# Sharing the split of a weight block between context and latent columns, moving the scans, and moving residual additions to VectorE

## The chip, the cores and the metric

The kernel runs on one core of a Trainium2 chip. Its time is the device time of one execution in microseconds (us). Five engines work from queues of their own and meet at semaphores: TensorE (PE, with the weight load PEld), VectorE (DVE), ScalarE (ACT), GpSimd (POOL) and SyncE (SP), which issues most DMA transfers. A queue runs in order: an instruction that waits holds up all that stand behind it.

## The reference

One layer of a hybrid block over 2048 latent tokens of width 1024, with a prefix of 256 context tokens that shares the weights. The parts that the change touches:

```python
hc = modulate(rms_norm(ctx, g_pre_mix[l]), sm_c, cm_c)           # 256 context tokens
_, _, xs_c, B_c, C_c, dt_c = mixer_inputs(hc, w_in[l], ..., full=False)
y_c, hf_c, hb_c = ssd_bidir(xs_c, B_c, C_c, dt_c, ..., h0, h0, False)   # gives the start states
hx = modulate(rms_norm(x, g_pre_mix[l]), sm_x, cm_x)             # 2048 latent tokens
uf_x, z_x, xs_x, B_x, C_x, dt_x = mixer_inputs(hx, w_in[l], ..., full=True)
y_x, _, _ = ssd_bidir(xs_x, B_x, C_x, dt_x, ..., hf_c, hb_c, True)
x = x + gm_x * rms_norm(mixer_output(...), g_post_mix[l])
hx2 = modulate(rms_norm(x, g_pre_ffn[l]), sf_x, cf_x)
x = x + gf_x * rms_norm(swiglu(hx2, w_gate[l], w_up[l], w_down[l]), g_post_ffn[l])
```

`mixer_inputs` multiplies by `w_in` and passes the x, B and C columns through a convolution of seven taps along a row. The scan of the latent tokens starts from the final states of the context.

## The kernel before, in words

**Numbers.** A float32 product is made of three fast matmuls: each factor is split into a high part (`hi`, a cast) and a low part (`lo`, the subtraction of the high part), and hi·hi, hi·lo and lo·hi are summed in PSUM. So each weight block costs a load of 512 KB (`wload`, tile `raw`, four buffers), a cast and a subtraction (`wparts`, which names the engines).

**Projection (some 90 to 720 us).** Tokens come in three sections: 0 and 1 are the two halves of the latent tokens (1024 each), 2 is the context (256). The list `blocks` holds, in order, which 128 columns (kind z, u, x, B, C or dt, and number) are multiplied for which section. A block of section 0 or 1 is 48 matmuls of 512 columns, one of section 2 is 24 of 256. While block n is multiplied, `want` loads the weights of block n+2, and when it ends `finish_block` starts their split and the block's own chain (`column_block`: convolution on VectorE, Silu on ScalarE, transposes on TensorE, a store). When one of the next two blocks is of the context, the low part is made on VectorE, and a latent block's cast too; otherwise the low part is on GpSimd and the cast on ScalarE. PSUM has three places for blocks, handed round in turn; a place is free when the convolution has read it.

Side chains run between the matmuls, set in order by a planner (`Pace`): each step of a chain has a due time in planned TensorE time and is written into the queues when that time has come; `drain` writes the rest of a chain at once. Such chains are: `dt_section` (the step sizes of a section, some twenty short VectorE instructions), `scan_steps` (states from chunk to chunk; section 2 first, its end state starts section 0), `section_chain` (loads, normalizes and modulates 512 rows of section 1), `ada_steps` and `fourier_steps`.

**FFN.** Gate and up products follow, then `down`: two passes p of seven positions each. A position is 11 blocks of 12 matmuls; `down_parts` makes each block's two operands (`wd` and `hd`, a cast on ScalarE and a subtraction on VectorE each), four blocks ahead. In the product numbered 6, `block(11)` is first replaced in place by `block(12)` minus `block(11)`. `finish` scales four row tiles and adds the residual rows, in eight pairs of half tiles, beside the following position; it runs three times (pass 0 position 6, pass 1 positions 0 and 5). From the second gate and up pass on, the order of each queue is made by the compiler's list scheduler, not by hand.

Of the kernel before, what the change touches and what calls it, by code (L numbers as in the profile page):

```python
# [17 lines left out]
ALU = mybir.AluOpType  # L18
# [12 lines left out]
XB, BB, CB, ZB = 6, 4, 4, 6  # L31
# [133 lines left out]
def fourier_ssd_block(ctx, tc, a):  # L165
# [624 lines left out]
    def group(kind, sec):  # L790
        return [(kind, j, sec) for j in range({"z": ZB, "u": 2, "x": XB, "B": BB, "C": CB}[kind])]

    c_, light = group("B", 2) + group("x", 2), group("z", 0)[4:] + group("u", 0)
    blocks = group("z", 0)[:4] + [("dt", 0, 2)]
    for i, blk in enumerate(light + group("B", 0)):
        blocks += c_[i : i + 1] + [blk]
    blocks += c_[8:]
    x_ = group("x", 0)
    blocks += x_[:5] + [("dt", 0, 0)] + x_[5:] + group("C", 0)
    u_, b_, x_, z_ = group("u", 1), group("B", 1), group("x", 1), group("z", 1)  # L800
    cl = group("C", 1)
    blocks += u_ + [("dt", 0, 1)] + b_ + x_
# [6 lines left out]

    wraw, wq = {}, {}  # L810

    def want(bi):
        if bi < len(blocks) and blocks[bi][0] != "dt":
            kind, j, sec = blocks[bi]
            c0 = off[kind] + j * P
            wraw[bi] = wload(w_in[:, :, c0 : c0 + P], [P, KD, P])

    def split(bi, *engines, **where):
        if bi in wraw:
            wq[bi] = wparts(wraw.pop(bi), [P, KD, P], *engines, **where)  # L820
        yield

# [115 lines left out]
    def down_parts(p, i, f):  # L938

        hpos[1] = (7 * p + i) * ((NJ + 1) // 2) + f // 2  # L940
        hidden_loads(3 if f % 2 == 0 else 2)

        def block(b):
            return wblock[p, (b, f // 4)][:, f % 4]

        def temp():
            return ta[0].tile([P, 512], F32, tag="ws", name="wt", bufs=4)

        def sub(engine, out, x, y):
            engine.tensor_tensor(out, x, y, op=ALU.subtract)  # L950
            return out

        i_ = ORDER[p][i]
        if i_ in (1, 5):
            src = block(11)
        elif i_ in (2, 3):
            src = block({2: 21, 3: 22}[i_])
        elif i_ == 6:
            sub(G, block(11), block(12), block(11))
            src = sub(V, temp(), block(22), block(11))  # L960
        elif i_ == 7:
            src = sub(G, temp(), block(22), block(12))
        else:
            src = sub(G, temp(), block(11), block(22))
            V.tensor_tensor(src, src, block(21), op=ALU.add)
        w = wp.tile([P, 2, 512], F32R, tag=("hi", "lo")[pos[1] % 2], name="wd")
        S.copy(w[:, 0], src)
        sub(V, w[:, 1], src, w[:, 0].bitcast(F32))
        raw = hraw[7 * p + i, f // 2][:, f % 2]
        tag, bufs = (("xt", 2), ("sg", 3))[pos[1] // 2 % 2]  # L970
        h = ta[0].tile([P, 2, 512], F32R, tag=tag, name="hd", bufs=bufs)
        S.copy(h[:, 0], raw)
        sub(V, h[:, 1], raw, h[:, 0].bitcast(F32))
        return w, h
# [427 lines left out]
    with tc.manual_schedule(engines=ordered):  # L1402
# [136 lines left out]
        def when(ready, gen):  # L1539
            while not ready():  # L1540
                yield 0.5
            yield from gen

        def settled(kinds, sec):
            return all(b in chains and chains[b].done for b in range(2, nblk) if blocks[b][0] in kinds and blocks[b][2] == sec)

        def finish_block(bi, ps):
            kind, j, sec = blocks[bi]
            live = [chains[b] for b in plain if b in chains and not chains[b].done and (blocks[b][2] == 2) == (sec == 2)]
            pace.drain(*live[:-1])  # L1550
            two = after(bi, 2)
            brief = two < nblk and any(blocks[b][2] == 2 for b in (after(bi, 1), two))
            splits[two] = pace.start(split(two, *((V, V) if brief and blocks[two][2] != 2 else (V,) if brief else (G,))))
            chains[bi] = pace.start(column_block(kind, j, sec, ps.rearrange("p a b -> p (a b)"), lambda: read.add(bi)))
# [11 lines left out]
        while bi < nblk:  # L1566
            kind, j, sec = blocks[bi]
            if kind == "dt":
                pace.drain(*[chains[b] for b in chains if blocks[b][0] == "dt"])
                if sec == 0:  # L1570
                    pace.drain(scan[2])
                chains[bi] = pace.start(dt_section(acts[sec], sec, place(bi), lambda bi=bi: read.add(bi)))
                pace.due()
                bi += 1
                continue
            want(after(bi, 2))
            pace.drain(splits[bi])
            pace.now = max(pace.now, splits[bi].t)
            if (kind, j, sec) == ("x", 1, 0):
                prep1[0] = pace.start(section_chain(0, lambda: True))  # L1580
            if (kind, j, sec) == ("C", 0, 0):
                pace.drain(prep1[0])
                prep1[1] = pace.start(section_chain(1, lambda: 1 in begun))
            if bi == first1:
                b1 = after(bi, 1)
                want(after(bi, 3))
                pz = [place(bi), place(b1)]
                pace.drain(splits[b1])
                for i, b in ((0, bi), (0, b1), (1, bi), (1, b1)):
                    if i == 1 and b == bi:  # L1590
                        pace.drain(prep1[1])
                    for k in range(KD):
                        project_step(pz[b - bi], wq[b], acts[1][i], i, k)
                        pace.due()
                    if i == 1:
                        finish_block(b, pz[b - bi])
                fnet = pace.start(when(lambda: settled("u", 1), fourier_steps()))
                late.append(pace.start(when(lambda: fnet.done, load_wo(0, "B"))))
                bi += 2
                continue  # L1600
            if bi == plain[-3]:
                pace.window = None
                pace.drain(ada)
                pace.drain(*[chains[b] for b in chains if blocks[b][0] != "z"], scan[1])
                places[1] = 1
                vacate("y")
                begin_outputs()
                pend.append(chunk_loads(NCH - 1, False))
                front = pace.start(chunk_front(pend[0]), 5.0)
                wts = pace.start(when(lambda: fnet.done, late_steps()), 1.0)  # L1610
            if bi == plain[-2]:
                pace.hurry = True
                pace.drain(*late)
                wo_raw.extend(wo_load(1, kp) for kp in range(KD // 2))
            if bi == plain[-1]:
                pace.due()
                pace.drain(fnet, front, wts)
                wo1 = load_wo(1, "C")
            if after(bi, 1) == first1:
                ps = project(bi, wq.pop(bi), acts[sec], lambda: begun.update({1: True}))  # L1620
            elif bi == plain[-1]:
                ps = project(bi, wq.pop(bi), acts[sec], beside=wo1)
            else:
                ps = project(bi, wq.pop(bi), acts[sec])
            finish_block(bi, ps)
            if kind == "x" and j == XB - 1:
                scan[sec] = pace.start(when(lambda sec=sec: settled("xB", sec), scan_steps(sec)), 8.0)
            bi += 1
        fourier_split(pend[0])
        pace.window = None  # L1630
# [219 lines left out]
    def finish(p, r, o, sq):  # L1850

        ss = ta[0].tile([P, 4], F32, tag="fss", name="fss", bufs=2)
        V.tensor_tensor(ss, sq[:, :, 0], sq[:, :, 1], op=ALU.add)
        rs = []
        for _ in rsqrt_steps(ss, 4, 1.0 / D, rs):
            yield
        for t in range(4):
            for n in range(2):
                oh = o[:, t, half[n]]
                V.scalar_tensor_tensor(oh, oh, rs[0][:, t : t + 1], gffn[n], ALU.mult, ALU.mult)  # L1860
                G.tensor_tensor(oh, oh, ff.x2[:, t, half[n]], op=ALU.add)
                yield
        b = PAIRS[p][r]
        dma(out_d[4 * b * P : 4 * (b + 1) * P, :].rearrange("(t p) d -> p t d", p=P), o)
# [42 lines left out]
    def down(p, prev):  # L1907
# [3 lines left out]
        for pos_, i in enumerate(order):  # L1911
# [9 lines left out]
            while f < NJ:  # L1921
# [7 lines left out]
                for ff_ in range(f, f + m):  # L1929
                    if (pos_, ff_) in at:  # L1930
                        down_load(*at[pos_, ff_])
                    steps(run, 2)
                    if (pos_, ff_) in rows:
                        rows_load(p, rows[pos_, ff_])
                f += m
# [64 lines left out]
```

## Time and profile before

| | |
|---|---|
| Time, median of 3 runs | 2375.2 us (2374.72 to 2376.2) |
| The profiled execution's own time | 2376.4 us |
| Span of its instructions | 2374.6 us |
| PE busy in the span | 2261.2 us (95%), 10861 matmuls |
| DVE, ACT, POOL busy | 1557.1, 1079.6, 999.8 us |
| Mean granted clock of TensorE | 0.984 |

A granted clock of 1.00 is 2.4 GHz and 0.50 is 1.2 GHz. In rows of a timeline the columns are the start, the duration, the engine, the line, the operation, output and inputs by their names in the program, the shape and the count; idle time of the engine before it and what ended that stand in brackets.

### The profile page before, as it was taken

What the parts mean: (1) busy time and instruction counts of PE and PEld (TensorE: products, weight loads), DVE (VectorE), ACT (ScalarE), POOL (GpSimd) and SP (SyncE); (2) the same over time, 40 slices, a digit from 0 to 9 for tenths busy, and PEclk for the clock granted to TensorE, in tenths of its full rate; (3) what the DMA queues carried; (4) which work ended last, traced back from release to release, by engine and by line L of the source; (5) the groups of instructions that cost most, each with busy time, mean ns of one, the idle gap of its engine ahead of it and who ended that gap; (6) DMA issues with size and microseconds to landing.
All of it is one profiled execution on the core that took longest, in us unless ns stands there. A gap on an engine that the chain in (4) does not pass through costs nothing. (4 is left out here: it accounts for less than half of the span.)

```text
span 2374.6 us, 30049 instructions
## 1 busy us (share of the span) xinstructions
PE 2261.2 (95%) x10861; PEld 1854.2 (78%) x10861; DVE 1557.1 (66%) x2202; ACT 1079.6 (45%) x1978; POOL 999.8 (42%) x659
## 2 busy tenths in 40 slices
PE   7998998999999999988999999999999999998998
PEld 3887777777788888866888887788888878876786
DVE  3557766567557888886655556755555565779766
ACT  4433553345247777756432323332333335444454
POOL 2121526424433444434555464445454532325512
PEclk9999999999999999999999999999999999999999
DMA  9455536354687888733332332433333373547233
GB/s 308 136 161 158 160 93 227 121 157 135 195 276 219 258 252 255 245 122 116 115 102 98 103 102 93 164 111 98 111 106 102 119 268 93 195 153 255 88 124 120
DMA packets 272291, 375.02 MB, mean 158 GB/s; under 512 B 17079, under 2 KB 190211, under 8 KB 269326
## 3 DMA queue, kind: packets, MB, share of 16 engines
q1 hardware_dynamic: 242486, 342.32, 45.3%
q10 hardware_dynamic: 29656, 30.78, 3.8%
q8 instruction: 86, 1.41, 0.2%
q14 instruction: 63, 0.52, 0.1%
HBM read 278.33 MB, written 94.72 MB: 157 GB/s over the span
## 5 line engine op out<-in xcount | busy, mean ns | idle before, releaser
L143 PE MATMUL b<-wd,hd 128*128 128x512 f32 x1848 | 429.2, 394 | 16.1 <-DVE hd L143 10.8
L143 PEld LDWEIGHTS b<-wd,hd 128*128 128x128 f32 x1848 | 349.9, 190 | 95.2 <-DVE hd L143 13.4
L143 PE MATMUL mm<-slot,wa 128*128 128x512 f32 x1584 | 378.4, 392 | 10.5 <-ACT sg L143 6.9
L143 PEld LDWEIGHTS mm<-slot,wa 128*128 128x128 f32 x1584 | 297.5, 189 | 75.6 <-ACT sg L143 7.7
L143 POOL TENSOR_TENSOR ws<-raw 128x512 f32<-128x512 f32 x88 | 127.4, 1449 | 311.8 <-DMA raw<-in_w_up_dram 117.7
L143 PE MATMUL mm<-actC,wa 128*128 128x512 f32 x984 | 239.8, 392 | 7.5 <-DVE u L143 7.2
L143 PE MATMUL mm<-actB,wa 128*128 128x512 f32 x1020 | 239.3, 389 | 0.0
L143 ACT CAST wa<-ws 128x512 fp32r<-128x512 f32 x176 | 109.2, 621 | 253.2 <-PE mm L143 213.4
L143 PEld LDWEIGHTS mm<-actC,wa 128*128 128x128 f32 x984 | 185.4, 189 | 47.2 <-issue 8.8
L143 PEld LDWEIGHTS mm<-actB,wa 128*128 128x128 f32 x1020 | 191.2, 188 | 39.6
L143 DVE TENSOR_TENSOR wa<-ws,wa 128x512 fp32r<-128x512 f32 x176 | 154.4, 879 | 59.6 <-ACT wa L143 56.7
L143 PE MATMUL mm<-actA,hi 128*128 128x512 f32 x512 | 165.9, 405 | 9.6 <-DVE acc L143 6.4
L143 DVE SCALAR_TENSOR_TENSOR acc<-mm,convw,acc 128x1008 f32<-128x1008 f32 (+3 forms) x156 | 161.9, 1040 | 19.5 <-ACT acc L143 16.5
L143 POOL TENSOR_TENSOR lo<-raw,hi 128x1024 fp32r<-128x1024 f32 x34 | 81.8, 2407 | 204.4 <-ACT hi L143 200.8
L143 DVE TENSOR_TENSOR u<-u,mm 128x512 f32<-128x512 f32 x126 | 86.5, 687 | 116.4 <-PE mm L143 116.3
L143 DVE TENSOR_TENSOR wa<-raw,wa 128x512 fp32r<-128x512 f32 x132 | 120.1, 911 | 64.5 <-ACT wa L143 64.0
L143 POOL TENSOR_TENSOR rq_y<-rq_ms,mhalf 128x1 f32<-128x1 f32 (+2 forms) x60 | 41.2, 691 | 284.3 <-DVE rq_ms L143 265.8
L143 ACT CAST wa<-raw 128x512 fp32r<-128x512 f32 x132 | 82.3, 624 | 161.9 <-PE mm L143 147.3
L143 POOL TENSOR_TENSOR adacc<-adacc,adaw 128x1024 f32<-128x1024 f32 x28 | 68.3, 2439 | 136.8 <-ACT adaw L143 136.8
L143 DVE TENSOR_TENSOR hd<-hraw,hd 128x512 fp32r<-128x512 f32 x154 | 117.3, 764 | 8.3 <-ACT hd L143 8.3
L143 PEld LDWEIGHTS mm<-actA,hi 128*128 128x128 f32 x512 | 95.1, 192 | 33.2 <-DVE acc L143 6.6
L143 ACT ACTIVATE ab<-ab,lda 128x128 f32<-128x128 f32 x384 | 118.8, 391 | 0.4 <-ACT sz L143 0.4
(309 smaller groups left out, 4534.6 us busy)
## 6 DMA issues: line engine op xcount, KB each, us to landing
hraw<-hg SPq DMA_DIRECT2D x70, 512.0 KB
raw<-in_w_in_dram SPq DMA_DIRECT2D x54, 512.0 KB
ab<-acsd SPq DMA_DIRECT2D x128, 192.0 KB
raw<-in_w_gate_dram SPq DMA_DIRECT2D x44, 512.0 KB
raw<-in_w_up_dram SPq DMA_DIRECT2D x44, 512.0 KB
hg<-hs SPq DMA_DIRECT2D x22, 1024.0 KB
adaw<-in_w_ada_dram SPq DMA_DIRECT2D x32, 512.0 KB
l_x<-xtok SPq DMA_DIRECT2D x33, 384.0 KB
```

The source lines that it names most:

```text
L143: r = issue(out, *args, **kw)
```

## The change

The list `blocks` now holds, for each of the four B and six x blocks, the context's block and right behind it section 0's block of the same columns; after every second pair stands one of the blocks z4, z5, u0, u1. `shared` tells that a block has the weights of the one before it: then nothing is loaded or split, and the operands are used again. The dt block of section 0 stands after the second C block. The first `section_chain` starts at the block x5 of section 0 and the second at C3 (before: x1 and C0). The scans wait by `ready_to_scan`. In `down`, product 6 of pass 1 and the residual additions of `finish` go from GpSimd to VectorE, and one step of `finish` is written per block in place of two.

```diff
-    c_, light = group("B", 2) + group("x", 2), group("z", 0)[4:] + group("u", 0)
+    light, cl = group("z", 0)[4:] + group("u", 0), group("C", 0)
     blocks = group("z", 0)[:4] + [("dt", 0, 2)]
-    for i, blk in enumerate(light + group("B", 0)):
-        blocks += c_[i : i + 1] + [blk]
-    blocks += c_[8:]
-    x_ = group("x", 0)
-    blocks += x_[:5] + [("dt", 0, 0)] + x_[5:] + group("C", 0)
+    for i, (kind, j, _) in enumerate(group("B", 0) + group("x", 0)):
+        blocks += [(kind, j, 2), (kind, j, 0)] + (light[i // 2 : i // 2 + 1] if i % 2 else [])
+    blocks += cl[:2] + [("dt", 0, 0)] + cl[2:]
...
+    def shared(bi):
+        return bi > 0 and blocks[bi - 1][0] != "dt" and blocks[bi] == (*blocks[bi - 1][:2], 0) and blocks[bi - 1][2] == 2
     def want(bi):
-        if bi < len(blocks) and blocks[bi][0] != "dt":
+        if bi < len(blocks) and blocks[bi][0] != "dt" and not shared(bi):
...
-        if bi in wraw:
+        if bi < len(blocks) and shared(bi):
+            wq[bi] = wq[bi - 1]
+        elif bi in wraw:
...
-            sub(G, block(11), block(12), block(11))
+            sub(V if p else G, block(11), block(12), block(11))
...
+        def ready_to_scan(sec):
+            dt_done = any(chains[b].done for b in chains if blocks[b] == ("dt", 0, sec))
+            return settled("xB", sec) and dt_done and (sec == 2 or scan[2].done)
...
-            if (kind, j, sec) == ("x", 1, 0):
+            if (kind, j, sec) == ("x", XB - 1, 0):
                 prep1[0] = pace.start(section_chain(0, lambda: True))
-            if (kind, j, sec) == ("C", 0, 0):
+            if (kind, j, sec) == ("C", CB - 1, 0):
                 pace.drain(prep1[0])
                 prep1[1] = pace.start(section_chain(1, lambda: 1 in begun))
...
-                late.append(pace.start(when(lambda: fnet.done, load_wo(0, "B"))))
+                late.append(pace.start(when(lambda: fnet.done and ada.done, load_wo(0, "B"))))
...
-                scan[sec] = pace.start(when(lambda sec=sec: settled("xB", sec), scan_steps(sec)), 8.0)
+                scan[sec] = pace.start(when(lambda sec=sec: ready_to_scan(sec), scan_steps(sec)), 8.0)
...
-                G.tensor_tensor(oh, oh, ff.x2[:, t, half[n]], op=ALU.add)
+                V.tensor_tensor(oh, oh, ff.x2[:, t, half[n]], op=ALU.add)
...
-                    steps(run, 2)
+                    steps(run, 1)
```

## Rows read from the trace of the kernel before

**Rows 1.** Waits of PE, 200 to 430 us: total, times, longest.
```profile
PE mm L143 <- DVE acc L143: 6.4, 1, 6.4
PE a L143 <- ACT v L143: 6.3, 1, 6.3
PE a L143 <- DVE dtp L143: 4.1, 1, 4.1
PE a L143 <- DVE h L143: 2.4, 1, 2.4
```

**Rows 2.** Windows over two low-clock stretches: each engine's busy us, clock, DMA.
```profile
224.70:231.50 6.80, 5.71 (x16) 4.55 (x16) 6.44 (x13) 4.35 (x6) 2.38 (x1) 0.50 0.26 88
388.50:398.80 10.30, 5.85 (x15) 4.88 (x16) 4.03 (x6) 3.77 (x4) 7.75 (x5) 0.50 0.81 267
```

**Rows 3.** Windows, one per position of down (PE, PEld, DVE, ACT, POOL, clock).
```profile
2075.17:2105.09 29.92, 29.92 (x134) 24.77 (x132) 16.73 (x26) 15.07 (x31) 0.00 (x0) 1.00 0.52 168
2105.09:2138.25 33.16, 30.80 (x133) 24.55 (x132) 28.87 (x34) 13.37 (x26) 17.59 (x11) 1.00 0.40 138
2138.25:2181.53 43.28, 35.20 (x133) 27.55 (x132) 42.00 (x42) 17.17 (x34) 29.38 (x18) 0.88 0.70 259
2181.53:2211.45 29.92, 29.92 (x133) 24.78 (x132) 19.04 (x30) 12.89 (x24) 10.04 (x6) 1.00 0.52 166
...
2303.07:2334.78 31.71, 30.22 (x133) 24.70 (x132) 31.20 (x38) 15.08 (x31) 15.11 (x9) 1.00 0.40 137
```

**Rows 4.** Timeline of POOL and DVE around the end of one finish.
```profile
2123.44 3.41 POOL L143 TENSOR_TENSOR slot<-slot,actC 128x512 f32<-128x512 f32 x2 [1.29 <-DVE slot L143]
2123.95 1.77 DVE L143 TENSOR_TENSOR wd<-actB,wd 128x512 fp32r<-128x512 f32 x1
...
2127.93 0.68 DVE L143 TENSOR_TENSOR wd<-slot,wd 128x512 fp32r<-128x512 f32 x1
```

**Rows 5.** POOL's groups, 2105 to 2182 us: count, busy us, mean ns.
```profile
L143 POOL TENSOR_TENSOR slot<-slot,actC 128x512 f32<-128x512 f32 x16 | 27.1, 1715 | 4.7 <-DVE slot L143 3.8 <-issue 0.9
L143 POOL TENSOR_TENSOR actC<-actA,actC 128x512 f32<-128x512 f32 x8 | 12.6, 1577 | 13.1 <-DVE wd L143 13.1
```

**Rows 6.** DVE's groups by form in the projection, 154.7 to 198.4 us.
```profile
L143 DVE TENSOR_TENSOR lo<-raw,hi 128x1024 fp32r<-128x1024 f32 x7 | 8.6, 1225 | 1.8 <-ACT hi L143 1.4
L143 DVE SCALAR_TENSOR_TENSOR acc<-mm,convw,acc 128x1008 f32<-128x1008 f32 x4 | 5.0, 1261 | 0.0
...
L143 DVE SCALAR_TENSOR_TENSOR acc<-mm,convw,acc 128x254 f32<-128x254 f32 x4 | 1.9, 482 | 0.1
```

**Rows 7.** Window over one pair of a context and a latent block.
```profile
168.80:183.06 14.26, 14.26 (x78) 12.24 (x77) 13.82 (x17) 5.45 (x7) 2.40 (x1) 1.00 0.61 184
```

**Rows 8.** Timelines: second preparation of section 1 (square, scaling, first and seventh transposes).
```profile
335.68 1.04 ACT L143 ACTIVATE junk<-xt 128x1024 bf16<-128x1024 f32 x1
...
351.42 2.75 DVE L143 TENSOR_SCALAR xt<-xt,rq_y 128x1024 f32<-128x1024 f32 x4
...
374.81 1.03 PE L143 MATMUL a<-ident,xt 128*128 128x128 f32 x8
...
384.56 0.60 PE L143 MATMUL a<-ident,xt 128*128 128x128 f32 x4
```

**Rows 9.** Timelines: first preparation of section 1 (first square, last transposes).
```profile
247.38 1.04 ACT L143 ACTIVATE junk<-xt 128x1024 bf16<-128x1024 f32 x1
...
284.07 0.60 PE L143 MATMUL a<-ident,xt 128*128 128x128 f32 x4
```

**Rows 10.** Timeline of PE: first and last state matmuls of the context's scan.
```profile
258.86 1.46 PE L143 MATMUL a<-xd,l_b 128*128 128x192 f32 x8
...
285.89 1.46 PE L143 MATMUL a<-xd,l_b 128*128 128x192 f32 x8
```

**Rows 11.** Timelines: SP's store after a finish, and ACT's first copy of the next position.
```profile
2168.81 0.55 SPq L1864 DMA_DIRECT2D out_dram<-slot  x1
...
2177.71 0.59 ACT L143 COPY slot<-b 128x512 f32<-128x512 f32 x1 [0.27 <-PE b L143]
```

More of the change, by code (lines that the diff above doesn't have):

```diff
@@ L1619, in fourier_ssd_block @@
             if after(bi, 1) == first1:
-                ps = project(bi, wq.pop(bi), acts[sec], lambda: begun.update({1: True}))
+                ps = project(bi, wq[bi], acts[sec], lambda: begun.update({1: True}))
             elif bi == plain[-1]:
-                ps = project(bi, wq.pop(bi), acts[sec], beside=wo1)
+                ps = project(bi, wq[bi], acts[sec], beside=wo1)
             else:
-                ps = project(bi, wq.pop(bi), acts[sec])
+                ps = project(bi, wq[bi], acts[sec])
             finish_block(bi, ps)
             if kind == "x" and j == XB - 1:
-                scan[sec] = pace.start(when(lambda sec=sec: settled("xB", sec), scan_steps(sec)), 8.0)
+                scan[sec] = pace.start(when(lambda sec=sec: ready_to_scan(sec), scan_steps(sec)), 8.0)
             bi += 1
```

## The prediction

> **What bounds the kernel now.** I looked first at the windows of every 25 us, to see where TensorE is not busy: it is nearly full in the middle, so time can come only from its holes. Two regions of the change have holes. In the projection the waits of TensorE add up to 19.2 us between 200 and 430 us, in four pieces: 6.4 us before block x0 of section 0, 2.4 us at the context's scan and the first preparation of section 1, 4.1 us in the dt chain, 6.3 us at the first pair of section 1 [rows 1]. The two long ones cost more than the hole: the granted clock then stands at 0.50, which is 1.2 GHz, for 6.8 and 10.3 us [rows 2]. Half of TensorE's busy time in there is lost: 5.71/2 = 2.9 us and 5.85/2 = 2.9 us. So the hole before x0 costs 9.2 us and that at the pair 9.2 us.
>
> In the down stage I read one window per position. An undisturbed one takes 29.92 us; the three beside which a `finish` runs take 33.16, 43.28 and 31.71 us [rows 3]. They lose 3.2 + 13.4 + 1.8 = 18.4 us together. VectorE was busy 42.00 of the 43.28 us with 42 instructions, 1.00 us each; undisturbed, 26 instructions took 16.73 us, 0.64 us each [rows 3]. The timeline says why: a subtraction of two SBUF tiles takes 0.68 us alone and 1.77 us while GpSimd adds [rows 4]. The bound is VectorE slowed by GpSimd, not TensorE, in these positions.
>
> **The change, part by part.**
>
> *Ten splits fewer.* Ten loads, ten casts and ten subtractions of section 0's B and x blocks go. In the pairs before, VectorE was the full engine: 13.82 us busy of 14.26 us [rows 7]. After, a pair keeps six latent taps at about 1.26 us, six context taps at 0.48 us and one low part at 1.23 us [rows 6]: 7.6 + 2.9 + 1.2 = 11.7 us, against the 14.26 us that the pair takes on TensorE; after every second pair a z or u block without convolution gives VectorE more room. Then no place in PSUM is late, and the 9.2 us before x0 go. From below: nothing goes, if x0's place is late for another reason; but the wait names the convolution itself. I take -9. The loads and casts are worth nothing by themselves, since TensorE waits for no weights in rows 1.
>
> *The first preparation of section 1 and the context's scan* now run together beside x5, C0 and C1, as they did beside x1 to x3. The 2.4 us hole goes with them; I take +1 for less room, and 26 us at most (the rival on the scan).
>
> *The dt chain* again has two blocks beside it (C2, C3 in place of x5, C0): 4.1 us stay, 0.
>
> *The second preparation starts three blocks later*, and this is where I expect a new wait. Before, from the first square at 335.68 us to the scaled rows at 354.17 us it took 18.5 us; then it waited 20.6 us for its place, and seven of its eight transposes and modulations ran from 374.81 to 385.16 us, 10.4 us [rows 8]. After, it starts at C3, and TensorE needs its result after C3 and the two first halves of the pair, some 22 us later (each block is 10.9 us: a pair of 14.26 us, less 24 context matmuls, about 3 us, and its transposes). The planner allows 7 us for the load, so by these rows it is done at 7 + 18.5 + 10.4 = 36 us: 14 us late. But the 18.5 us hold the 4.1 us dt wait and 3.2 us of low clock, and steps written before the pair's end can run beside its matmuls: without the two it is 6.6 us. Bounds: 0 (rows in time, as before), and 22 us (as slow as the first preparation, 247.38 to 284.67 us = 37.3 us [rows 9], plus 7, less 22). I take 10 us between the two near values, and 3 us for the clock as in rows 2: 13 us in place of the 9.2 us at the pair, so +4. Queued behind the waiting transposes on TensorE are the second halves of the pair and section 0's scan; what is late next is block B0 of section 1, by the same amount.
>
> *The scan of section 0* waits for the dt chain and starts some two blocks later; its steps stay ahead of the Fourier part, and 0 is taken. *Waiting for `ada`* before the output weights: 0, they were loaded after it already.
>
> *Residual sums on VectorE.* GpSimd loses 24 additions, of which 16 took 1.72 us each [rows 5], and VectorE gains 24 at about 0.68 us [rows 4]. What goes is the slowing: all other instructions of the position fall from 1.00 to 0.64 us. Position by position, VectorE then needs (34 + 8) x 0.64 = 27 us of 29.92 in the first and (38 + 8) x 0.64 = 29.4 us in the third: they fit, the third barely. *Product 6 on VectorE*: GpSimd took 1.58 us each beside the finish [rows 5]; VectorE takes eleven in the second finish's position and the next. Over the two VectorE has 42 + 8 + 30 + 11 = 91 instructions x 0.64 = 58.2 us, in 59.84 us of TensorE. It fits over both, but not at the boundary: three blocks' subtractions and products stand in the first position too, 42 + 8 + 3 = 53 x 0.64 = 34 us for 29.92 us, 4 us late, partly covered by the four blocks (10.9 us) that are prepared ahead. I leave 4.4 us of the loss there and 1 us in the third: -13. Bounds: all 18.4 us gone, or only a quarter.
>
> By the Trainium skill ("VectorE: DVE Perf Modes", section "The DRAIN you can't avoid") a next instruction does not start until the pipe of the one before it is empty. By that each of the 91 would take its full 0.69 us, 62.8 us, and VectorE would be 3 us too slow for the two positions; the sum would be 3 us higher. The rows of the undisturbed position have 26 in 16.73 us, less than 0.69 us each, so the sum goes by 0.64.
>
> *One step of `finish` per block.* The store of 2 MB is written last and so goes later: it was issued at 2168.81 us and ScalarE's copy into the same tile's place began at 2177.71 us without waiting for it [rows 11], so it lands within 8.9 us. Issued at a position's end it could hold that copy, behind it the casts of the next weights on ScalarE, and behind the store on SP the `hraw` loads. The list scheduler can put the casts first; 0, at most 8.9 us less the 8.2 us of three prepared blocks.
>
> *Sum*: -9 + 1 + 4 - 13 = -17 us. The profiled span is 2374.6 us, the execution around it 2376.4 us, and the median of the runs 2375.2 us; the difference is taken from the median: **2358 us**.
>
> **The rivals.**
>
> *The preparation is in time* (chance 0.20). The planner's own sequence has it done near the need, and without the dt wait the rows give 6.6 us, which the first halves could hide. Then the +4 goes and the 9.2 us at the pair too: 2358 - 13 = 2345 us.
>
> *The preparation decides* (0.14). The first preparation took 37.3 us with the context's scan beside it [rows 9]; the second now has section 0's scan and the dt chain. 22 + 3 - 9.2 = +16 in place of +4: 2370 us.
>
> *VectorE becomes the bound of the down stage* (0.12). For it speaks 34 us of work for 29.92; against it the lead of four blocks. Only a quarter of the 18.4 us comes, and 2358 + 8 = 2366 us.
>
> *The context's scan is drained into TensorE's queue* (0.08), on the other side. The dt block of section 0 drains it, and now stands three blocks behind x5 of the context in place of five. From the first to the last state matmul it takes 28.5 us, of which TensorE works 4 x 1.46 = 5.8 us [rows 10]. If nothing of it has run by the dt block, TensorE waits 22.7 us and 3 us for the clock: 26 in place of 1, 2383 us. With 15 us of wait the time is that of before, and from 20 us it is slower by 0.2%. Against it: the planner gives it 33 us of blocks before that.
>
> *The change does nothing measurable* would need gains and the new wait to cancel, and is part of the same band.
>
> **How the numbers follow.** Forecast 0.46, the rivals as above. 0.2% of 2375 us, about what a measurement of this kernel can tell from no change, is 4.8 us. Faster than 2370.4 us are the forecast, the first and third rivals and a part of the second: 0.46 + 0.20 + 0.12 + 0.05 = 0.83. The rest of the second is within the bound: 0.09. Slower: 0.08. The forecast's own range is 2350 to 2366 us, by the bounds of the preparation's two near values and of the down stage. The range of all cases leaves out the drained scan and the slow end of the second rival: 2342 to 2371 us.
>
> **What would show it.** Right: 44 loads of `in_w_in` in place of 54; no wait of TensorE for `acc` before x0, and no VectorE cast `hi<-raw` there; the three positions beside a `finish` near 30, 34 and 31 us, VectorE's subtractions at 0.69 us throughout, GpSimd without `slot<-slot,actC`; a wait of some 10 us for `xt` or the modulated rows at the first pair of section 1. Wrong: that wait missing or above 20 us; several state matmuls of the context's scan in a row before the dt block with holes between; TensorE waiting for `hd` or `wd` at the start of pass 1 position 1, with VectorE full; ScalarE's copy waiting for the store.

## The result and the profile after

The changed kernel takes 2351.8 us (median of four runs, 2350.1 to 2354.4) where the kernel before takes 2375.6 us on the same chip (2374.7 to 2376.2): 23.8 us less, ratio 0.9901, 95% interval 0.9884 to 0.9918. The forecast was 2358 us with a range of 2342 to 2371, faster. Sign and range are right; the forecast is 6 us too high, and the terms behind it are not equally good. The profiled execution takes 2351.9 us, its span is 2350.1 us, at a mean granted clock of 0.986. One execution of 8214.89 us in the set of two steps and one of 2561.26 us of the kernel before in the third set stand far from the others and are left out of the ratios.

The page: busy time, share of the span and instructions of each engine, and the loads of `in_w_in`.

```profile
PE 2260.1 (96%) x10861; PEld 1852.8 (79%) x10861; DVE 1529.5 (65%) x2220; ACT 1080.3 (46%) x1977; POOL 939.5 (40%) x623
...
raw<-in_w_in_dram SPq DMA_DIRECT2D x44, 512.0 KB
```

TensorE's work is the same, VectorE has 27.6 us less and GpSimd 60.3 us less; the 44 loads are as forecast. The waits of TensorE from 200 to 430 us, which answer to [rows 1]:

```profile
PE a L143 <- DVE h L143: 5.1, 2, 3.4
PE a L143 <- DVE dtp L143: 4.0, 1, 4.0
PE a L143 <- POOL xd L143: 2.5, 1, 2.5
PE a L143 <- DVE xt L143: 1.9, 3, 1.2
PE a L143 <- DVE br L143: 1.1, 1, 1.1
```

The wait for `acc`, a block's convolution, before x0 is gone. The wait for `dtp`, the step sizes of the dt chain, stays. `h` is the state that a scan carries on: at the context's scan TensorE now waits 3.4 us for it, at 318 us, where it waited 2.4 us. `br` is a row of the `ada` chain; its wait of 1.1 us at 331 us holds the last state matmuls of the context's scan, and before there was one of 0.7 us at 213 us. The rest stands at the first pair of section 1, its first two blocks, whose first halves are multiplied ahead of the second ones: `xt` are the rows that a preparation scales, `xd` the weighted rows that section 0's scan multiplies, and 1.7 us of `h` are that scan's. Windows (columns as in [rows 2]): first the whole stretch of the first six pairs and two single blocks, then four stretches of low clock.

```profile
94.63:205.81 111.18, 111.18 (x587) 95.09 (x585) 64.83 (x92) 47.63 (x63) 24.07 (x10) 1.00 0.41 126
...
319.26:322.68 3.42, 3.42 (x10) 2.72 (x10) 2.59 (x4) 1.19 (x2) 1.28 (x1) 0.52 0.61 223
363.63:367.05 3.42, 3.42 (x10) 2.65 (x9) 3.31 (x5) 2.62 (x5) 0.00 (x0) 0.52 0.02 5
384.12:387.53 3.41, 3.10 (x13) 2.36 (x13) 2.00 (x5) 2.07 (x3) 0.22 (x1) 0.52 0.00 0
390.94:397.77 6.83, 5.05 (x23) 4.02 (x21) 4.76 (x6) 1.55 (x2) 5.11 (x4) 0.51 0.77 237
```

In the first line TensorE is busy for all of 111.18 us: these pairs hold nothing up. The others say where the clock still falls to 1.2 GHz: behind the scan's wait, behind the dt chain and twice at the first pair of section 1. The windows of the down stage, one per position, answer to [rows 3] (last of pass 0; positions 0, 1 and 5 of pass 1):

```profile
2098.18:2128.37 30.19, 30.19 (x134) 24.70 (x132) 28.85 (x48) 15.15 (x31) 1.02 (x1) 1.00 0.59 196
2128.37:2158.29 29.92, 29.92 (x134) 24.77 (x132) 28.79 (x49) 15.41 (x30) 2.59 (x1) 1.00 0.77 282
2158.29:2188.21 29.92, 29.92 (x134) 24.77 (x132) 22.08 (x36) 12.94 (x24) 10.06 (x6) 1.00 0.65 213
2279.89:2309.81 29.92, 29.92 (x134) 24.77 (x132) 27.64 (x46) 15.08 (x31) 1.50 (x1) 1.00 0.50 163
```

The three positions beside a `finish` took 33.16, 43.28 and 31.71 us [rows 3] and now take 30.19, 29.92 and 29.92: of 18.4 us lost, 0.3 us are left. VectorE has more instructions (48, 49 and 46 for 34, 42 and 38) and is busy no longer, 0.59 to 0.60 us each. Its timeline around a boundary, which answers to [rows 4], and a group of the first window:

```profile
2124.39 0.69 DVE L143 TENSOR_TENSOR hd<-hraw,hd 128x512 fp32r<-128x512 f32 x1
2124.99 0.68 DVE L143 TENSOR_TENSOR slot<-slot,b 128x512 f32<-128x512 f32 x1
2125.59 0.68 DVE L143 TENSOR_TENSOR actC<-actA,actC 128x512 f32<-128x512 f32 x1
...
L143 DVE TENSOR_TENSOR actC<-actA,actC 128x512 f32<-128x512 f32 x2 | 1.4, 684 | 0.0
```

No instruction of VectorE in these four windows takes 0.78 us or more, where the longest took 1.79 us before. While none waits, one starts every 0.60 us. The last line shows two subtractions of product 6 (`actC<-actA,actC`) that run in the last position of pass 0; before, GpSimd made two of them there too.

### The profile page after: what moved, and what is told of

It is laid out like the page before. It is cut to its first block, busy times and chain, and to the rows that moved or that the text cites. A ratio compares the mean times of both kernels' runs of the same rounds, so it can differ in the third digit from the quotient of the medians.

```text
span 2350.1 us, 29965 instructions
## 1 busy us (share of the span) xinstructions
PE 2260.1 (96%) x10861; PEld 1852.8 (79%) x10861; DVE 1529.5 (65%) x2220; ACT 1080.3 (46%) x1977; POOL 939.5 (40%) x623
## 5 line engine op out<-in xcount | busy, mean ns | idle before, releaser
L143 PE MATMUL b<-wd,hd 128*128 128x512 f32 x1848 | 421.5, 390 | 4.0 <-ACT hd L143 1.8
L143 PE MATMUL mm<-slot,wa 128*128 128x512 f32 x1584 | 381.4, 394 | 10.5 <-ACT sg L143 6.9
L143 PEld LDWEIGHTS mm<-actA,hi 128*128 128x128 f32 x512 | 94.0, 190 | 25.4 <-issue 3.4
L143 DVE TENSOR_TENSOR hd<-hraw,hd 128x512 fp32r<-128x512 f32 x154 | 108.7, 707 | 5.8 <-ACT hd L143 5.8
```

Of the source, the lines that this page charges most:

```text
L143: r = issue(out, *args, **kw)
```

## The experiments

Each kernel's difference is its median less the median of the kernel before on the same chip (2374.0 us in the first two sets, 2375.1 and 2374.1 us in the others); by the same measure the change itself is -23.8 us. An interval of a ratio is about 0.0015 to either side, 3.6 us, so differences between two experiments of under 5 us are read from profiles or left open. Spans are those of the profiles, and two profiles of the same code differ too: the five traces with the projection as changed reach the gate and up stage at 1027.1 to 1030.7 us, the two with the projection as before at 1032.8 and 1036.5 us.

**The down stage alone** (the kernel before with these lines).

```diff
-            sub(G, block(11), block(12), block(11))
+            sub(V if p else G, block(11), block(12), block(11))
...
-                G.tensor_tensor(oh, oh, ff.x2[:, t, half[n]], op=ALU.add)
+                V.tensor_tensor(oh, oh, ff.x2[:, t, half[n]], op=ALU.add)
...
-                    steps(run, 2)
+                    steps(run, 1)
```

> The kernel before with the three edits of the down stage alone (residual sums and product 6 of pass 1 on VectorE, one step per block). If the down stage's gain is its own, its three positions beside a finish fall from 33.2, 43.3 and 31.7 us to about 30 each, 18 us of 2375.6: 2357 to 2358 us, and the waits of TensorE between 200 and 430 us stay 19 us. The rival, that both halves of the change give back part of each other's gain (the later stage merely takes up what the earlier one left), expects under 14 us.

2355.7 us, -18.3; ratio 0.9923 (0.9908 to 0.9938). The three positions take 30.25, 29.92 and 29.90 us. All of the stage's gain stands without the projection's part.

**The projection alone** (the changed kernel with those lines put back).

> The changed kernel with the down stage as before. The projection's net gain alone: the trace of the changed kernel is 11.1 us ahead at the first B block of section 1 and 9.1 us at its end, so 2364 to 2371 us, with the three positions at 33, 43 and 32 us again. If the down stage's loss hung on the state in which the projection leaves the queues, the positions come out otherwise.

2370.6 us, -3.4; ratio 0.9986 (0.9976 to 0.9996). The positions take 33.20, 43.50 and 31.70 us again. The two parts give -21.7 us in sum, the change -23.8: within the intervals they add. Most of the diff's lines are worth 3 us, three lines in `down` 18.

**Residual sums back on GpSimd**, the rest as changed.

```diff
-                V.tensor_tensor(oh, oh, ff.x2[:, t, half[n]], op=ALU.add)
+                G.tensor_tensor(oh, oh, ff.x2[:, t, half[n]], op=ALU.add)
```

> The changed kernel with the residual sums back on GpSimd alone (product 6 stays on VectorE, one step per block). If GpSimd's additions slow VectorE, subtractions beside them take 1.77 us again and the positions lose most of the 18 us: pass 1 position 0 at 36 us or more, 2362 to 2370 us. If the spreading to one step per block was what helped, the loss stays under 5 us.

2362.2 us, -11.8; ratio 0.9948 (0.9933 to 0.9963). The windows of the three positions, and VectorE's costliest group in the second:

```profile
2099.86:2131.72 31.86, 30.52 (x134) 24.62 (x132) 31.34 (x39) 14.01 (x28) 14.65 (x9) 1.00 0.44 142
2131.72:2167.86 36.14, 32.38 (x133) 25.69 (x132) 35.12 (x46) 16.55 (x32) 16.21 (x9) 0.95 0.79 287
2289.44:2321.33 31.89, 30.23 (x133) 24.70 (x132) 31.39 (x38) 15.07 (x31) 15.18 (x9) 1.00 0.45 144
...
L143 DVE TENSOR_TENSOR hd<-hraw,hd 128x512 fp32r<-128x512 f32 x10 | 11.1, 1115 | 0.0
```

VectorE has three instructions fewer than in the changed kernel in the second position and is busy 6.3 us longer: the low part that takes 0.68 us alone takes 1.1 us on the mean. Fewer instructions on VectorE, and more time for them: the bound is the slowing.

**Product 6 back on GpSimd**, the rest as changed.

```diff
-            sub(V if p else G, block(11), block(12), block(11))
+            sub(G, block(11), block(12), block(11))
```

> The changed kernel with product 6 of pass 1 back on GpSimd alone. Eleven subtractions of 1.6 us run beside the second finish and slow about as many VectorE instructions by 1.1 us, 9 to 12 us of VectorE; with the sums on VectorE it needs 42 + 8 instructions there, 32 us, plus this: pass 1 position 0 at 33 to 40 us, 3 to 10 us lost. The rival, that VectorE has room for it since it runs four blocks ahead, expects under 2 us.

2355.7 us, -18.3; ratio 0.9924 (0.991 to 0.9939). Position 0 of pass 1, and GpSimd's and VectorE's groups in it:

```profile
2127.11:2161.27 34.16, 30.60 (x133) 24.62 (x132) 33.46 (x42) 16.04 (x32) 15.90 (x10) 1.00 0.62 219
...
L143 POOL TENSOR_TENSOR actC<-actA,actC 128x512 f32<-128x512 f32 x6 | 9.5, 1590 | 10.2 <-DVE wd L143 10.2
...
L143 DVE TENSOR_TENSOR hd<-hraw,hd 128x512 fp32r<-128x512 f32 x10 | 9.0, 898 | 0.0
```

The same mechanism: VectorE has 42 instructions in place of 49 and needs 33.46 us for them in place of 28.79, and the position loses 4.2 us. The additions put back cost 12.0 us and product 6 put back 5.5 us, 17.5 of the 18.3 us.

**Two steps of `finish` per block**, the rest as changed.

```diff
-                    steps(run, 1)
+                    steps(run, 2)
```

> The changed kernel with two steps of finish per block, as before. The list scheduler orders the queues by readiness, and VectorE has the same work: under 2 us either way if the spreading does nothing; 3 us or more lost in the three positions if it is what keeps the operands in time.

2352.2 us (median of three), -21.8; ratio 0.9903 (0.9887 to 0.992), span 2350.9 us for 2350.1. The three positions take 30.19, 29.92 and 29.92 us. Once GpSimd is out of the way, this edit does nothing that can be measured.

**The order without the sharing.** Every block loads and splits its own weights again.

```diff
-        return bi > 0 and blocks[bi - 1][0] != "dt" and blocks[bi] == (*blocks[bi - 1][:2], 0) and blocks[bi - 1][2] == 2
+        return False and bi > 0 and blocks[bi - 1][0] != "dt" and blocks[bi] == (*blocks[bi - 1][:2], 0) and blocks[bi - 1][2] == 2
```

> The changed kernel, its order kept, but each latent block of a pair loads and splits its own weights again. If the work of the ten splits on VectorE was the cause of the hole before x0, VectorE is full again in the pairs (13 to 14 us busy of 14.3) and holes for the convolution come back, 6 to 15 us lost in all: 2358 to 2367 us. If the order of the blocks (convolutions spread over all of section 0, a z or u block after every second pair) is what removed it, the time stays within 4 us of 2351.8.

2361.9 us, -12.0; ratio 0.995 (0.9935 to 0.9964): 11.8 us worse than with the sharing. The time lies where the load theory expected it, but the loss does not lie in the pairs, where that theory and the prediction put it. The window of the first six pairs and two single blocks in this kernel, and (second fence) that of the stretch ahead of x0 in the kernel before:

```profile
94.10:205.80 111.70, 111.70 (x589) 95.50 (x587) 75.26 (x103) 48.26 (x64) 23.98 (x10) 1.00 0.52 154
```

```profile
154.70:225.79 71.09, 64.00 (x351) 53.81 (x349) 57.96 (x66) 26.01 (x36) 9.62 (x4) 0.99 0.60 175
```

With the six splits of these pairs back, VectorE has 75.26 us of work in 111.70 us, and TensorE does not wait for a moment; x5 starts at 278.4 us as in the changed kernel (278.6). In the kernel before, VectorE's work is bunched: 57.96 of 71.09 us in four pairs without a single block between them and the two context blocks behind them. So the order is enough to remove the hole before x0. What is lost without the sharing is lost later: from the start of C0 to the start of C3 this kernel takes 70.9 us for 63.1, and in section 1 TensorE waits 12.9 us for `acc` where it waits 8.0 us. In the first of these stretches both kernels cast and subtract the same blocks, so their load does not explain it; how the sharing changes the written order there was not separated.

**The second preparation begins at C2** in place of C3.

```diff
-            if (kind, j, sec) == ("C", CB - 1, 0):
+            if (kind, j, sec) == ("C", CB - 2, 0):
```

> The changed kernel with the second preparation of section 1 started one block earlier, at C2. If its late start makes the waits for scaled rows at the first pair (1.9 us of holes and part of the low clock there), these go and the time falls by 2 to 6 us. If the pair is held by the scan of section 0 and the dt chain, nothing changes by more than 2 us.

2345.7 us, -28.3; ratio 0.9882 (0.9868 to 0.9897); span 2342.9 us, 7.2 less. No wait for `xt` is left at the first pair, block B0 of section 1 starts at 411.6 us for 417.4, and the gate and up stage at 1022.7 for 1027.2. The late start costs 4.5 us by the medians, about the size of what two intervals leave open; the run with the first preparation at x4, below, has the same ratio. The 7.2 us of the spans say too much: the stretch from the gate and up stage to the down stage, which this edit leaves alone, takes 887.4 us in the changed kernel's trace and 882.5 to 884.6 us in the other traces.

**It begins at C1** (`CB - 3`).

> The kernel after with the second preparation of section 1 begun at C1 in place of C3. Theory (what its late start cost was the wait for the scaled rows, and that is gone when it begins at C2): nothing more, 2345.7 us within 3, no wait of TensorE for the rows at the first pair. Rival 1 (still late, and queued ahead of section 0's scan): another 3 to 6 us less, 2341 us. Rival 2 (it must wait for the first preparation, which begins at x5, and for its tiles): TensorE is held before C1 and 2350 us or more.

2349.7 us, -25.4; ratio 0.9892 (0.9877 to 0.9907). The two waits of TensorE between 280 and 430 us that tell it:

```profile
PE a L143 <- ACT hdec L143: 5.2, 1, 5.2
PE a L143 <- DVE h L143: 4.7, 2, 3.3
```

The rows are nearly in time (0.7 us of waits for `xt`), and TensorE waits 5.2 us at the last transposes for ScalarE (`hdec` holds the decay factors of the scan); beside the context's scan its four long waits add up to 7.2 us, for 4.8 in the changed kernel. The result lies between the theory and the second rival: earlier is not better. That the preparation meets the other chains fits these waits, but was not tried apart.

**The dt block of section 0 after C0** in place of C1.

```diff
-    blocks += cl[:2] + [("dt", 0, 0)] + cl[2:]
+    blocks += cl[:1] + [("dt", 0, 0)] + cl[1:]
```

> The kernel after with section 0's dt block one block earlier, after C0 in place of C1. It drains the context's scan, of which 16 of 32 state matmuls then stand in a row before it. Theory (the rival on the drained scan, in part): the scan makes eight matmuls in about 9 us, so TensorE waits for the second 16 some 10 to 18 us, plus 3 us of low clock, and gives little back: 2362 us or more. Rival: section 0's scan, which waits for dt, begins a block earlier and less of it stands beside section 1's convolutions: 2348 us or less.

2373.0 us, -2.1; ratio 0.9993 (0.9983 to 1.0003): 21.7 us lost by one place in a list. TensorE's timeline before the dt block and at the next hole:

```profile
302.95 1.57 PE L143 MATMUL a<-xd,l_b 128*128 128x192 f32 x8 [2.07 <-POOL xd L143]
306.18 1.57 PE L143 MATMUL a<-xd,l_b 128*128 128x192 f32 x8 [1.66 <-POOL xd L143]
309.42 1.57 PE L143 MATMUL a<-xd,l_b 128*128 128x192 f32 x8 [1.67 <-POOL xd L143]
313.16 1.57 PE L143 MATMUL a<-xd,l_b 128*128 128x192 f32 x8 [2.17 <-POOL xd L143]
...
346.84 1.22 PE L143 MATMUL mm<-actA,hi 128*128 128x512 f32 x2 [5.58 <-DVE acc L143]
```

The dt block drains the context's scan, and TensorE's queue then holds the scan's matmuls with a hole ahead of each group: 7.6 us in four waits, not the 10 to 18 that were expected. The remainder goes with what is late behind it in the trace: 5.58 us for a convolution, 4.1 us for a cast at 384 us, and three stretches of low clock of 6.8 to 13.7 us between 345 and 414 us.

**The first preparation one block earlier**, at x4, the second at C2.

```diff
-            if (kind, j, sec) == ("x", XB - 1, 0):
+            if (kind, j, sec) == ("x", XB - 2, 0):
```

> The kernel after with the second preparation begun at C2, as in the run that did this alone (ratio 0.9882), and the first preparation begun one block earlier, at x4 of section 0 in place of x5. In that run TensorE lost 3.4 + 1.1 us and 1.7 us of low clock, 6.2 us, between 316 and 333 us, beside the context's scan and the first preparation. Theory (VectorE has the scan's steps and the preparation's at one place, and the loss goes with their overlap): with the squares and the scaling done beside the last pair, the holes after C0 go in good part and the ratio falls by 3 to 6 us, to some 0.986. Rival (the holes are the scan's own step from state to state, which the preparation does not set): the first preparation ends earlier, the same holes for the state stay, and the ratio is 0.988 within 0.001.

2347.5 us, -26.6; ratio 0.9882 (0.9865 to 0.9898), as at C2 alone. The four executions spread from 2343.8 to 2350.5 us, and the profile is of one at the upper end. Waits of TensorE from 290 to 355 us:

```profile
PE a L143 <- POOL xd L143: 3.8, 2, 2.2
PE y L143 <- DVE acc L143: 0.6, 1, 0.6
PE a L143 <- ACT tok L143: 0.5, 1, 0.5
```

The wait for `h` is gone and one for `xd`, another step of the same scan, stands in its place; C3 starts at 353.7 us for 352.9. The rival holds in the time, though not in its words that the same holes stay: the waits there add up to about as much (4.9 us for 4.8), under other names. This speaks for the scan's own pace and against its overlap with the preparation.

**Another cure for the kernel before.** Its order is kept; beside the context, the latent blocks' casts go to ScalarE and their low parts to GpSimd.

```diff
-            splits[two] = pace.start(split(two, *((V, V) if brief and blocks[two][2] != 2 else (V,) if brief else (G,))))
+            splits[two] = pace.start(split(two, *((V,) if brief and blocks[two][2] == 2 else (G,))))
```

> The kernel before, its order kept, with the splits of latent blocks next to a context block taken from VectorE (cast to ScalarE, low part to GpSimd) and nothing else. If VectorE being full in the pairs makes the hole before x0, it goes or shrinks below 2 us and with the low clock behind it 6 to 9 us come: 2366 to 2370 us. If the hole is due to the order (two context blocks in a row before x0), it stays.

2358.1 us, -15.9; ratio 0.9929 (0.9912 to 0.9945): by the medians more than four times what the changed projection gives. The stretch up to x0, and the wait there:

```profile
157.80:227.85 70.05, 64.57 (x350) 53.67 (x349) 49.53 (x57) 29.26 (x40) 19.88 (x9) 1.00 0.54 163
...
PE mm L143 <- DVE acc L143: 3.3, 1, 3.3
```

VectorE is busy 49.53 of 70.05 us, the hole before x0 shrinks from 6.4 to 3.3 us, and the one at the first pair is gone. The theory expected less than 2 us of that hole and 6 to 9 us of gain, the rival an unchanged hole: neither holds, so in the old order the load has a part in the hole and what is left of it has another cause. Some 10 to 12 us of the gain lie between the start of block B0 of section 1 and the first matmul of the gate and up stage (596 us, for 608 and 606.5 in the two traces with the old projection), where the edit changes no split.

**That cure and the down stage together.**

> The kernel before, its order of blocks kept, with the latent blocks' casts and low parts beside the context taken off VectorE and with the three edits of the down stage. Theory: the two gains lie in different stages and add, -15.9 and -18.3 us: 2374.0 - 34.2 = 2339.8 us, span near 2338, and the three positions near 30 us. Rival: part of the 15.9 us came from what the down stage gives back, since the lighter GpSimd and VectorE move the work between stages: 2344 us or more, with the start of the down stage later than the 1902 us of the run with the split edit alone.

2338.1 us, -36.9; ratio 0.9843 (0.9829 to 0.9858): 13 us less than the changed kernel (by the two differences), the fastest of all here. The sum of its parts is -34.2. Waits of TensorE from 430 to 720 us, first in this kernel, then in the kernel before:

```profile
PE a L143 <- DVE h L143: 2.5, 1, 2.5
PE a L143 <- ACT acc L143: 1.3, 1, 1.3
PE a L143 <- POOL xd L143: 1.1, 1, 1.1
```

```profile
PE a L143 <- ACT acc L143: 8.6, 4, 4.0
PE a L143 <- issue: 2.6, 2, 1.8
PE a L143 <- DVE h L143: 2.2, 1, 2.2
PE mm L143 <- DVE acc L143: 2.0, 1, 2.0
```

In section 1 the waits for `acc` fall from 8.6 to 1.3 us. Why a lighter section 0 leaves section 1 in better step is not settled: the planner writes another sequence, and its parts were not tried one by one.

## Why the prediction was right, and where it was not

**The hole before x0, -9: the size is right, the cause is not.** The hole is gone, 9.2 us. "Ten splits fewer" was named as the reason, with 11.7 us of VectorE per pair. The window of six pairs and two single blocks has 64.83/6 = 10.8 us per pair, so the load was well sized; but the kernel without sharing has no hole there either. The new order, with single blocks between the pairs, is enough by itself; what the sharing would do in the old order was not tried. The lighter splits come near to it: ahead of x0 they take four casts and five low parts off VectorE, as the sharing would, and half of the hole stayed. So the size came right by a term that did not need its reason, which is luck.

**The first preparation and the context's scan, +1: measured +4.1.** TensorE waits 3.4 + 0.3 + 1.1 us, and half of the 3.42 us at low clock is lost: 6.5 us in place of 2.4. Of the 1.1 us for `br` some 0.7 us may be only moved, from 213 us. It looks like a small dose of the rival on the drained scan: the dt block stands three blocks behind the context's x5, and one block less costs 21.7 us. That rival's wait was too dear: it took the scan's 28.5 us from [rows 10], where the scan is spread between other work; drained, it makes eight matmuls every 3.2 to 3.7 us. That its total of 26 us is near the 21.7 us is luck: two thirds of those stand behind the wait, where the rival counted 3 us.

**The dt chain, 0: measured -1.6.** 4.0 us and 1.7 us of low clock, for 4.1 and 6.37/2 = 3.2 us (PE busy in the low stretch from 330.50 us before).

**The second preparation, +4: the lateness is right, its price is not.** ScalarE, VectorE and TensorE at the first pair:

```profile
366.44 1.04 ACT L143 ACTIVATE junk<-xt 128x1024 bf16<-128x1024 f32 x1
...
382.30 2.07 DVE L143 TENSOR_SCALAR xt<-xt,rq_y 128x1024 f32<-128x1024 f32 x3
...
381.64 0.27 PE L143 MATMUL a<-ident,xt 128*128 128x128 f32 x1
383.10 0.33 PE L143 MATMUL a<-ident,xt 128*128 128x128 f32 x1 [1.19 <-DVE xt L143]
383.76 0.33 PE L143 MATMUL a<-ident,xt 128*128 128x128 f32 x1 [0.33 <-DVE xt L143]
384.42 3.31 PE L143 MATMUL a<-ident,xt 128*128 128x128 f32 x13 [0.33 <-DVE xt L143]
390.25 2.14 PE L143 MATMUL a<-xd,l_b 128*128 128x192 f32 x8 [2.51 <-POOL xd L143]
394.09 3.99 PE L143 MATMUL a<-ident,xt 128*128 128x128 f32 x16 [1.70 <-DVE h L143]
397.75 0.79 PE L143 MATMUL mm<-actA,hi 128*128 128x512 f32 x2
```

TensorE has finished the first halves at 381.6 us and gets to the second ones at 397.75 us: 16.1 us, near the 14 us that the rows gave. The wait for `xt` is there, but with 1.9 us, and all waits are 6.1 us; the other 4.2 us are for section 0's scan (`xd`, `h`). In the rest TensorE transposes and makes state matmuls of section 0, which it had to do anyway (32 transposes at 1.03/8 us and eight matmuls in 1.46 us, 5.6 us at full clock). Lost are 16.1 - 5.6 = 10.5 us, for 9.2 us at the pair before: about +1. The term took 10 us of wait and 3 of clock.

**The scan of section 0, 0: not measured apart.** 40 of its state matmuls, 0.18 us each [rows 10], stand behind the start of block B0 of section 1 instead of ahead of it (from 360 us to that start the group `a<-xd,l_b` has 16 matmuls in place of 56). Of the 11.1 us by which B0 starts earlier, 7 are therefore only moved. It fits that from there to the gate and up stage the five traces with the changed projection take 609.8 to 613.9 us, the two with the old one 606.5 and 607.9.

**The projection in sum, -4: measured -3.4** (-5.7 to -1.0 by the interval). The terms as the profile sizes them are -9.2 + 4.1 - 1.6 + 1.3 = -5.4. The term of the context's scan was 3.1 us too low, those of the second preparation and the dt chain 2.7 and 1.6 us too high: the sum is near because errors cancelled, which is luck.

**Residual sums and product 6, -13: mis-sized, measured -18.3 alone.** This is the step that made the forecast 6 us too high. The mechanism is as put, and its bound "all 18.4 us gone" is what came. The step counted 42 instructions in the last position of pass 0, 53 in position 0 of pass 1 (34 us for 29.92) and 91 - 53 = 38 in position 1, and left 4.4 us in position 0 and 1 us in the third. The three hold 48, 49 and 36: the sum of 133 was exact, but six more than counted run in the last position of pass 0, where there was room: four that came there from the next position and two subtractions of product 6 that had stood there on GpSimd, which the step's eleven for the two later positions overlooked. And each took 0.59 to 0.60 us in these full positions, not the 0.64 of a position with idle time between the instructions. So the 49 needed 28.79 us of 29.92, and nothing was late at the boundary.

The prediction's other price, 3 us more by the Trainium skill, rests on half of what the section says. The same place ("VectorE: DVE Perf Modes", section "The DRAIN you can't avoid") adds: "A next op that is not held starts earlier". The trace agrees with that, with starts 0.60 us apart for durations of 0.68.

**Waiting for `ada`, one step of `finish`: 0.** The second was tried and is 0 within the interval; the first was not tried alone.

**The rivals.** The preparation in time (2345 us) was made by starting it at C2: 2345.7 us. VectorE as the bound of the down stage did not come. The preparation that decides did not come either. The drained scan did not come in the changed kernel; with the dt block one place earlier most of its price did.

## What to carry to other kernels

Where an engine is full, ask first what slows its instructions: moving a neighbour's work onto it can relieve it, and the price to count is the undisturbed one. A queue that fills up in bunches can be cured by spreading the heavy blocks, so try the order alone before crediting the saving. And before a block that drains another chain is moved, count how much of that chain is still unwritten there: one place in the order was worth 22 us here.

## What the runs showed of the hardware

A subtraction of two 128x512 SBUF tiles on VectorE lasts 0.68 us and starts 0.60 us after the one before it, when nothing disturbs it. Beside GpSimd the mean of the low part `hd<-hraw,hd` rises to 0.90 us (product 6 back on GpSimd, nine of its subtractions in a position of 34 us) and 1.12 us (residual sums back on GpSimd, eight of its additions in one of 36 us). The clock makes a hole dearer: behind the scan's wait of 3.4 us it stood at 1.2 GHz for 3.42 us, which cost 1.7 us, half as much again.
